# A two-layer encoder trunk on one core: where the modulation sums, the head's small rows and the last expert unit's combine are done

## The chip, the cores and the metric

The kernel runs on 1 core of one Trainium2 chip. The metric is the device time of one execution in microseconds (us), as the median of several runs. Engines are called as in the profile: PE (TensorE), DVE (VectorE), ACT (ScalarE), POOL (GpSimd), SP (SyncE, which here only issues DMAs); PEld is PE's weight load.

## What is computed

A sequence of 512 tokens with 1024 channels goes through two layers. Each layer has a mixer (layer 0: multi-scale pooling beside banded chunk attention; layer 1: a Mamba-2 state-space mixer with 8 groups) and a mixture of 32 experts, of which each token takes two. Every sub-layer is modulated by six rows of 1024 numbers, `mod`, which depend on one conditioning vector `c`. The reference, cut to what matters here:

```python
c_act = jax.nn.silu(c)                                   # (1, 1024)
for layer in range(2):
    mod = c_act @ ada_w[layer] + ada_b[layer]            # 1024 x 6144 weights
    shift1, scale1, gate1, shift2, scale2, gate2 = split(mod, 6)
    h = rmsnorm(x, norm1_w[layer]) * (1 + scale1) + shift1
    if layer == 0:
        u, q, k, v = split(h @ mix_w_in)
        mix = concat([pool_mixer(u), chunk_attention(q, k, v, rel_bias)]) @ mix_w_out
    else:
        mix = mamba2_mixer(h, ssm_w_in, conv_w, conv_b, dt_bias, A_log, D_skip, norm_w, w_out)
    x = x + gate1 * mix
    h2 = rmsnorm(x, norm2_w[layer]) * (1 + scale2) + shift2
    g = top-1 of softmax(h2 @ w_group + b_group)         # 4 groups of 8 experts
    w = top-2 of softmax of the logits inside group g    # two experts a token
    x = x + gate2 * sum_e w_e * (silu(h2 @ w1_e) * (h2 @ w3_e)) @ w2_e
return rmsnorm(x, final_norm_w)
```

## The kernel before

**The stages in order.** Head (x is loaded and normalized, the shift and scale of layer 0 are summed, the V columns of attention are formed); even mixer (scores, softmax, pooling, beside the Q, K and U columns, one 128-column strip at a time); output product and router; experts of layer 0 in 17 units; combine of layer 0, in which the last expert results are added to x, x is normalized and transposed into `sh_hi`, `sh_lo`, the input of layer 1; the SSM, 8 groups `g0` to `g7`, each of which forms the columns b, c, x, z of its group (PSUM tiles `pdb`, `pdc`, `pdx`, `pdz`), convolves them on DVE (`cvx`), and runs the scan (`pst`, `pyd`, `pyo`; `ms` are the decay masks); output product and router; experts of layer 1; combine and final norm.

**Modulation sums.** `ada(layer, part, eng)` (L164) forms 2048 numbers of `mod`: for each of 8 blocks `k` of 128 rows, a 1 MB tile `ada` of weights is loaded by SP into a ring of 5 buffers (tag w8), DVE multiplies it by column `k` of silu(c), `ccol`, and adds it to the running sum (L189), in place; then four matmuls with a stationary of ones (L198, PSUM tile `pada`) add over the 128 partitions, each into 32 partitions of one bank. It is a generator: each `yield` lets the caller put the next round where it wants. Five parts are formed so: (0,1), (0,2), (1,0) in the even mixer (table FILL says how many rounds go behind each piece of work) and (1,1), (1,2) in the SSM (list `fill`). The part (0,0) is formed in the head in two halves of 512 numbers twice (`ada_sums(b)`, L564), and the first four channels' blocks of h need half 0, the other four half 1 (`modulate(b)`).

**Head.** V products go in pairs of k: `wsplit` makes a high part of the weight on ACT and a low part on the engine of table LO ("v": POOL). `late_loads()` (L271) has SP load a zero row and three vectors of 32 numbers, each spread over 128 partitions: `dcol` (from ssm_D, with a stride of two elements, two DMAs), `dtb`, `arow`. Behind them in SP's queue stands `wq`, the first strip of Q columns, whose buffer is that of the V weights `vr4`.

**Experts and combine.** A unit u is 128 slots of one or two experts: PE forms `ph` and `pyy`, DVE scales the result into `y`, which SP stores to DRAM rows `yd`. The units of LAST and the overflow unit are not stored: their results are split in a high and a low half (`yh`, `yl`) and added to x by one-hot matmuls (`products`, L1073, operand `yot` or `yo`, PSUM tile `pyc`) and DVE adds (`padd`, L1086). The operand of unit 13 takes part in step u = 15 of the loop, those of 14 and 15 in `combine`. The stored results come back as 8 indirect DMAs of POOL that add into x (`ygather`, L1174, issued in unit GAT = 15). `combine` then follows an order written out by hand (STEPS; x0: add tile 0, h0: next step of its normalization, w1: split a weight). In layer 0 the call `ahead()` (L1433) ahead of it has SP load `wdt`, the 32 dt columns of the SSM weight, split on ACT and DVE into `whl`.

Of the kernel before, what the change touches and what calls it, by code (L numbers as in the profile page):

```python
# [20 lines left out]
P = 128  # L21
T = 512
# [14 lines left out]
GAT = 15  # L37
# [16 lines left out]
HOLD = 7  # L54
PINS = 3
# [7 lines left out]
LO = {"v": "G", "e": "VVG", "m": "V", "o": "GVV", "s": "VV"}  # L63
# [4 lines left out]
STEPS = "x0 h0 x1 h1 h0 x2 h2 h0 h1 x3 h2 h3 h3 h0 h1 h2 h1 w1 h3 w2 h3 h2"  # L68
# [7 lines left out]
def trunk_kernel(ctx, tc, x, c, ada_w, ada_b, norm1_w, norm2_w, mix_w_in, pool_w, pool_scale,  # L76
# [86 lines left out]

    def ada(layer, part, eng, first=None):  # L164
# [19 lines left out]
        load(1)  # L184
        for k in range(KD):
# [8 lines left out]
        for _ in range(SLACK):  # L194
            yield
        p = ps(name=f"pada{layer}{part}")
        for q in range(4):
            PE.matmul(p[32 * q:32 * q + 32, :], ones[:, 0:32], ws[KD - 1][:, q * 512:(q + 1) * 512], start=True,  # L198
                      stop=True, skip_group_check=True)
# [71 lines left out]
    def late_loads():  # L271
        SP.dma_start(yd[len(MAIN) * P:, :], zrow)
        for q in range(2):
# [216 lines left out]
    def even_mixer(layer):  # L490
        with ExitStack() as es:
# [15 lines left out]
            def ada_loads(b):  # L507
                SP.dma_start(adb[0:64:32, b * 512:(b + 1) * 512], dap(ada_b, b * 512, [[D, 2], [1, 512]]))
                for k in range(0, KD, 2):
# [3 lines left out]
                    aw[b, k], aw[b, k + 1] = (t[:, d].rearrange("p q n -> p (q n)") for d in range(2))  # L513
# [27 lines left out]
            def modulate(b):  # L541
# [12 lines left out]
            def v_products(b):  # L554
                for kk in (4 * b, 4 * b + 2):
# [8 lines left out]
            def ada_sums(b):  # L564
                V.tensor_scalar(aw[b, 0], aw[b, 0], ccol[:, 0:1], None, op0=ALU.mult)
                for k in range(1, KD):
                    V.scalar_tensor_tensor(aw[b, k], aw[b, k], ccol[:, k:k + 1], aw[b, k - 1], op0=ALU.mult,
                                           op1=ALU.add)
                p = ps(name=f"pada00{b}")
                for q in range(2):  # L570
                    PE.matmul(p[32 * q:32 * q + 32, :], ones[:, 0:32], aw[b, KD - 1][:, q * 512:(q + 1) * 512],
                              start=True, stop=True, skip_group_check=True)
                m = adb[0:64, b * 512:(b + 1) * 512]
                V.tensor_add(m, p[0:64], m)
                p = ps((P, 4, 64), name=f"pm00{b}")
                for q in range(4):
                    PE.transpose(p[:, q, :], m[:, q * P:(q + 1) * P], ident[0:64, 0:64])
                ks = slice(4 * b, 4 * b + 4)
                V.scalar_tensor_tensor(ab[:, 0, 0, ks], p[:, :, 32], 1.0, n1w[0][:, ks], op0=ALU.add, op1=ALU.mult)
                V.tensor_copy(ab[:, 0, 1, ks], p[:, :, 0])  # L580
# [3 lines left out]
            late_loads()  # L584
# [5 lines left out]
            v_products(1)  # L590
# [117 lines left out]
            adas = [ada(0, 1, V), ada(0, 2, V), ada(1, 0, V)]  # L708
# [81 lines left out]
    class Moe:  # L790
# [282 lines left out]
        def products(self, i, parts):  # L1073

            ps2 = [ps(name=f"pyc{self.layer}{i}{hf}") for hf in range(2)]
            for hf, p in enumerate(ps2):
                for n, part in enumerate(parts):
                    for q in range(2):
                        PE.matmul(p, part[2][:, i * P:(i + 1) * P], part[hf][:, q * 512:(q + 1) * 512],  # L1079
                                  start=n + q == 0, stop=n == len(parts) - 1 and q == 1)  # L1080
            return ps2
# [6 lines left out]
        def run(self, before_end=None):  # L1088
# [30 lines left out]
            def results(u, between=None):  # L1119
# [3 lines left out]
                             self.parts_y[max(u - NPAIR + 2, 0)] if last(u) else None)  # L1123

            ts = {}
            for u in range(NPAIR + 1):
# [20 lines left out]
                if 1 < u < NPAIR and last(u - 2):  # L1147
                    for i in range(NT):
                        self.padd(i, self.products(i, self.parts_y[:1]))
# [8 lines left out]
                if u == GAT:  # L1158
                    self.ygather()
                    for n in range(2):  # L1160
                        t = we([P, 2, 2 * T], F32R, f"yl{n}_{layer}")
                        o = we([P, 2, 2 * T], F32R, f"yo_{layer}")[:, 0, 0:T] if n else ot[:, T:2 * T]
                        self.parts_y.append((t[:, 0], t[:, 1], o))
                if u == 1:
# [256 lines left out]
    def odd_mixer(layer, prev):  # L1421
        with ExitStack() as es:
# [10 lines left out]
            def ahead():  # L1433
                dense.first = prev.gathers[HOLD]
                dense.load(2)
                w = prev.y_tile("wdt")
                wdt.append(w[:, 0:256].rearrange("p (k c) -> p k c", k=KD))
                SP.dma_start(wdt[0], w_in[:, 6144:6176].rearrange("(k p) c -> p k c", p=P))
                wdt.append(ws4(F32R, "whl")[:, 0:512].rearrange("p (k c) -> p k c", k=KD))
# [365 lines left out]
```

## Time and profile before

| | us |
|---|---|
| median of 3 runs | 1119.99 |
| lowest and highest run | 1119.96, 1123.87 |
| the profiled execution's own time | 1120.03 |
| its span in the trace | 1118.3 |
| PE busy in the span | 973.2 |
| DVE busy in the span | 800.3 |

The profiled execution's time is 1.7 us more than its span and 0.04 us from the median. Over the span PE is busy 87%, DVE 72%, ACT 35%, POOL 27%; the mean granted clock of TensorE is 0.932 of full speed, that is, it is at 1.2 GHz instead of 2.4 GHz in part of the span.

### The profile page before, as it was taken

What the parts mean: (1) busy time and instruction counts of PE and PEld (TensorE: products, weight loads), DVE (VectorE), ACT (ScalarE), POOL (GpSimd) and SP (SyncE); (2) the same over time, 40 slices, a digit from 0 to 9 for tenths busy, and PEclk for the clock granted to TensorE, in tenths of its full rate; (3) what the DMA queues carried; (4) which work ended last, traced back from release to release, by engine and by line L of the source; (5) the groups of instructions that cost most, each with busy time, mean ns of one, the idle gap of its engine ahead of it and who ended that gap; (6) DMA issues with size and microseconds to landing.
All of it is one profiled execution on the core that took longest, in us unless ns stands there. A gap on an engine that the chain in (4) does not pass through costs nothing. (4 is left out here: it accounts for less than half of the span.)

```text
span 1118.3 us, 15578 instructions
## 1 busy us (share of the span) xinstructions
PE 973.2 (87%) x5474; PEld 729.5 (65%) x5474; DVE 800.3 (72%) x1650; ACT 388.9 (35%) x753; POOL 300.2 (27%) x329
## 2 busy tenths in 40 slices
PE   4588788699699996898999899899989999799994
PEld 3466466388556654776786777777766878556653
DVE  6717986654565874789997989887797555564976
ACT  3135332425123232433444333443433325222332
POOL 4413100204231122411513416244142004231124
PEclk9789888799799998899999999999999999799997
DMA  9476876598699979536473465554334945699987
GB/s 332 139 265 168 286 282 252 215 364 330 209 364 414 411 229 255 210 107 198 143 264 88 135 194 159 190 158 113 126 109 152 333 154 209 204 390 415 412 278 185
DMA packets 140200, 263.88 MB, mean 236 GB/s; under 512 B 19917, under 2 KB 82337, under 8 KB 134994
## 3 DMA queue, kind: packets, MB, share of 16 engines
q1 hardware_dynamic: 129122, 235.40, 60.1%
q0 software_dynamic: 8928, 20.97, 7.2%
q10 hardware_dynamic: 2064, 6.42, 1.4%
q8 instruction: 47, 0.77, 0.3%
q14 instruction: 39, 0.32, 0.1%
HBM read 254.19 MB, written 20.11 MB: 245 GB/s over the span
## 5 line engine op out<-in xcount | busy, mean ns | idle before, releaser
L1036 PE MATMUL ph<-w,xT 128*64 128x256 f32 (+1 forms) x1152 | 132.1, 374 | 0.9 <-DVE xT L1020 0.7
L1036 PEld LDWEIGHTS ph<-w,xT 128*64 128x64 f32 x1152 | 86.8, 139 | 51.8 <-issue 10.9
L189 DVE SCALAR_TENSOR_TENSOR ada<-ada,ccol,ada 128x2048 f32<-128x2048 f32 x35 | 87.1, 2489 | 0.2
L1003 POOL DMA_INDIRECT xg<-xnd,toks x32 | 32.3, 1008 | 149.8 <-PE pxt L1015 122.6
L1057 PE MATMUL pyy<-w,hidT 128*64 128x512 f32 x272 | 65.9, 605 | 4.2 <-ACT hidT L1049 4.2
L1038 ACT ACTIVATE th<-ph 128x128 f32<-128x128 f32 x34 | 9.4, 278 | 160.8 <-PE pht L1047 137.1
L1022 ACT ACTIVATE xT<-pxt,mc 128x128 f32<-128x128 f32 x136 | 51.3, 458 | 17.9 <-PE pxt L1015 10.9
L1062 DVE SCALAR_TENSOR_TENSOR y<-pyy,wsl,gate 128x512 f32<-128x512 f32 x68 | 48.1, 744 | 6.1 <-DMA yd<-y 4.5
L1015 PE MATMUL pxt<-ident,xg 128*128 128x128 f32 x272 | 37.9, 284 | 15.5 <-DVEq L1383 7.9
L1086 DVE TENSOR_TENSOR x<-x,pyc 128x512 f32<-128x512 f32 x64 | 40.4, 682 | 14.1 <-PE pyc L1079 8.0
L1039 DVE SCALAR_TENSOR_TENSOR th<-th,ph 128x128 f32<-128x128 f32 x34 | 9.8, 287 | 55.7 <-ACT th L1038 55.7
L1020 DVE TENSOR_SCALAR xT<-pxt,mc 128x128 f32<-128x128 f32 x136 | 46.6, 405 | 1.4 <-PE pxt L1015 1.4
L1581 DVE TENSOR_SCALAR ms<-lb,acs 128x128 f32<-128x128 f32 x128 | 41.0, 359 | 5.9 <-DMA lb<-acd 3.6
L1015 PEld LDWEIGHTS pxt<-ident,xg 128*128 128x128 f32 x272 | 34.5, 194 | 16.2 <-issue 15.6
L1548 DVE SCALAR_TENSOR_TENSOR cvx<-pdx,cw,cvx 128x511 f32<-128x511 f32 (+2 forms) x48 | 35.4, 738 | 6.7 <-ACT cvx L1545 6.6
L1178 POOL DMA_INDIRECT x<-yd,row x16 | 25.1, 1571 | 50.0 <-DMA xgfw<-in_final_norm_w_dram 22.3
L1584 POOL TENSOR_TENSOR ms<-ms,cbm 128x512 f32<-128x512 f32 x16 | 32.0, 2001 | 17.8 <-ACT ms L1583 16.0
L1057 PEld LDWEIGHTS pyy<-w,hidT 128*64 128x64 f32 x272 | 16.5, 136 | 28.1 <-issue 19.4
L1079 PE MATMUL pyc<-yh,yot 128*128 128x512 f32 x128 | 33.7, 398 | 1.0 <-DVE yot L1070 1.0
L469 DVE TENSOR_TENSOR sor<-sor,gate 128x1024 f32<-128x1024 f32 x16 | 20.4, 1276 | 18.0 <-DMA sor<-in_ssm_w_out_dram 17.9
L661 ACT ACTIVATE scs<-scs,mx 128x512 f32<-128x512 f32 (+3 forms) x32 | 17.7, 555 | 36.2 <-DVE mx L660 32.8
L1079 PEld LDWEIGHTS pyc<-yh,yot 128*128 128x128 f32 x128 | 23.4, 188 | 9.6 <-issue 1.9
(1074 smaller groups left out, 2778.4 us busy)
## 6 DMA issues: line engine op xcount, KB each, us to landing
w<-in_moe_w_dram SPq DMA_DIRECT2D x192, 512.0 KB
ada<-in_ada_w_dram SPq DMA_DIRECT2D x40, 1024.0 KB
yd<-y SPq DMA_DIRECT2D x22, 512.0 KB
ada<-in_ada_w_dram SPq DMA_DIRECT2D x16, 512.0 KB
wx<-in_ssm_w_in_dram SPq DMA_DIRECT2D x16, 512.0 KB
wz<-in_ssm_w_in_dram SPq DMA_DIRECT2D x16, 512.0 KB
lb<-acd SPq DMA_DIRECT2D x32, 256.0 KB
sor<-in_ssm_w_out_dram SPq DMA_DIRECT2D x16, 512.0 KB
```

The lines of the kernel that those rows point to most:

```text
L189: a = eng.scalar_tensor_tensor(ws[k], ws[k], ccol[:, k:k + 1], ws[k - 1], op0=ALU.mult, op1=ALU.add)
L1003: d = GP.indirect_dma_start(out=xg, out_offset=None, in_=xnd[:, :], in_offset=bass.IndirectOffsetOnAxis(ap=idx, axis=0), bounds_check=T - ...
L1015: PE.transpose(p[:, q, :], xv[:, 4 * hf + q, :], ident)
L1020: V.tensor_scalar(xT[:, k, :], p[:, q, :], a, b, op0=ALU.mult, op1=ALU.add)
L1022: S.activation(xT[:, k, :], p[:, q, :], AF.Identity, bias=b, scale=a)
L1036: PE.matmul(ph[64 * j:64 * j + 64, n:n + h, :], xT[:, k, 64 * j:64 * j + 64], w13[n][:, :, k, :], start=k == 0, stop=k == KD - 1, skip_gro ...
L1057: PE.matmul(py[64 * j:64 * j + 64], hT[:, 64 * j:64 * j + 64], w2[:, s], start=True, stop=True, skip_group_check=True)
L1062: V.scalar_tensor_tensor(y[:, s], py, self.wsl[:, slot:slot + 1], self.gate2[:, s], op0=ALU.mult, op1=ALU.mult)
L1079: PE.matmul(p, part[2][:, i * P:(i + 1) * P], part[hf][:, q * 512:(q + 1) * 512], start=n + q == 0, stop=n == len(parts) - 1 and q == 1)
L1086: V.tensor_add(xst["x"][i][:, s], xst["x"][i][:, s], p)
L1548: V.scalar_tensor_tensor(a[:, sh:], p[:, :T - sh], cw[:, tap, ch:ch + 1], a[:, sh:], op0=ALU.mult, op1=ALU.add)
L1581: V.tensor_scalar(ms[:, h, :], lb[:, h, :], acs[:, cq, 4 * g + h:4 * g + h + 1], 0.0, op0=ALU.subtract, op1=ALU.min)
```

## The change

All modulation sums go to PE. A round k is four matmuls whose stationary is column k of `ccol`, broadcast to 32 columns, and whose moving operand is the loaded tile; they accumulate in the same PSUM bank from round 0 to round 7. DVE has no round any more. In the head the halves accumulate the same way, with the two k of a pair in different partitions, so one add more is needed behind the transposes. The vectors `dcol`, `dtb`, `arow` are loaded as three rows of [1, 32] into `hrow`, spread by one matmul with ones and copied by DVE (`head_rows`). The low parts of the V weights and all `hlo` go to DVE. The operand of unit 13 moves from step u = 15 to the final products, which become 64 matmuls in place of 48, and begin with three of the four operands for tiles 0 and 1; the gathers are issued in unit 14; in layer 0 `wdt` is loaded in unit 10 and split on ACT and POOL as a step `w0` of the combine.

```diff
-GAT = 15
+GAT = 14
+EARLY = 10
-LO = {"v": "G", "e": "VVG", "m": "V", "o": "GVV", "s": "VV"}
+LO = {"v": "V", "e": "VVG", "m": "V", "o": "GVV", "s": "VV"}
-STEPS = "... h3 h0 h1 h2 h1 w1 h3 w2 h3 h2"
+STEPS = "... h3 h0 h1 h2 h1 w0 w1 h3 w2 h3 h2"
+    def ada_mm(p, k, w, first, last):
+        for q in range(4):
+            PE.matmul(p[32 * q:32 * q + 32, :], ccol[:, k:k + 1].to_broadcast([P, 32]), w[:, q * 512:(q + 1) * 512],
+                      start=first, stop=last, skip_group_check=True)
...
+            if not eng:
+                if not k:
+                    p = ps(name=f"pada{layer}{part}")
+                ada_mm(p, k, ws.pop(k), k == 0, k == KD - 1)
+                continue
...
     def late_loads():
         SP.dma_start(yd[len(MAIN) * P:, :], zrow)
-        for q in range(2):
-            SP.dma_start(dcol[64 * q:64 * q + 64, :], dap(ssm_D, q, [[0, 64], [2, 16]]))
-        SP.dma_start(dtb, dap(ssm_dt_bias, 0, [[0, P], [1, 32]]))
-        SP.dma_start(arow, dap(ssm_A_log, 0, [[0, P], [1, 32]]))
+        hrow = st_.tile([1, 3, 32], F32, name="hrow")
+        for n, src in enumerate((ssm_D, ssm_dt_bias, ssm_A_log)):
+            SP.dma_start(hrow[:, n, :], dap(src, 0, [[0, 1], [1, 32]]))
...
-                    (V if g % 2 else GP).tensor_sub(parts[1][g], xa[g], parts[0][g].bitcast(F32))
+                    V.tensor_sub(parts[1][g], xa[g], parts[0][g].bitcast(F32))
...
             def ada_sums(b):
-                V.tensor_scalar(aw[b, 0], aw[b, 0], ccol[:, 0:1], None, op0=ALU.mult)
-                for k in range(1, KD):
-                    V.scalar_tensor_tensor(aw[b, k], aw[b, k], ccol[:, k:k + 1], aw[b, k - 1], op0=ALU.mult,
-                                           op1=ALU.add)
                 p = ps(name=f"pada00{b}")
-                for q in range(2):
-                    PE.matmul(p[32 * q:32 * q + 32, :], ones[:, 0:32], aw[b, KD - 1][:, q * 512:(q + 1) * 512],
-                              start=True, stop=True, skip_group_check=True)
+                for k in range(0, KD, 2):
+                    for d in range(2):
+                        for q in range(2):
+                            o = 64 * d + 32 * q
+                            PE.matmul(p[o:o + 32, :], ccol[:, k + d:k + d + 1].to_broadcast([P, 32]), aw[b, k][:, d, q],
+                                      start=k == 0, stop=k == KD - 2, skip_group_check=True)
...
-            adas = [ada(0, 1, V), ada(0, 2, V), ada(1, 0, V)]
+            adas = [ada(0, 1, None), ada(0, 2, None), ada(1, 0, None)]
...
-                             self.parts_y[max(u - NPAIR + 2, 0)] if last(u) else None)
+                             self.parts_y[max(u - NPAIR + 3, 0)] if last(u) else None)
...
-                if 1 < u < NPAIR and last(u - 2):
+                if 1 < u < NPAIR - 1 and last(u - 2):
...
-                p = [self.products(i, self.parts_y) for i in range(NT)]
+                p = self.products((0, 1), self.parts_y[:-1], False)
+                p = self.products((0, 1), self.parts_y[-1:], True, p)
+                p += self.products((2, 3), self.parts_y, True)
...
-                split(wdt[1][:, :, 0:32], wdt[1][:, :, 32:64], wdt[0], V)
+                split(wdt[1][:, :, 0:32], wdt[1][:, :, 32:64], wdt[0], GP)
...
-                a11, a12 = ada(1, 1, V, prev.gathers[HOLD]), ada(1, 2, V, prev.gathers[HOLD])
+                a11, a12 = ada(1, 1, None, prev.gathers[HOLD]), ada(1, 2, None, prev.gathers[HOLD])
```

What SP has in its queue in the head, behind the last V weights, before:

```order
L272 DMA yd<-zrow 1x1024
L274 DMA dcol<-in_ssm_D_dram 64x16x1 x2
L275 DMA dtb<-in_ssm_dt_bias_dram 128x32
L276 DMA arow<-in_ssm_A_log_dram 128x32
L402 DMA wq_498<-in_mix_w_in_dram 128x8x128
```

and now:

```order
L286 DMA yd<-zrow 1x1024
L289 DMA hrow<-in_ssm_D_dram 1x32
L289 DMA hrow<-in_ssm_dt_bias_dram 1x32
L289 DMA hrow<-in_ssm_A_log_dram 1x32
L425 DMA wq_522<-in_mix_w_in_dram 128x8x128
```

The four DMAs that write 128 partitions have become three that write one; `wq` stands behind them as before.

On PE, in the even mixer before the second U strip (`pdu` are the U columns): before, no sum stands here, and the first of the three parts has one row, behind the scores `sc` of a later strip:

```order
L655 MATMUL sc_965<-kT_891,qT_836 128x128
L655 MATMUL sc_974<-kT_891,qT_836 128x128
L198 MATMUL pada_983<-ada_732,ones 32x512 x4
L637 MATMUL py_1010<-pl_772,pw 128x512
L426 MATMUL pdq_1022<-hhi_176,q2h 128x512
```

Now five rounds of that part stand between the two U strips (the other three follow one at a time):

```order
L452 MATMUL pdu_709<-hhi_179,u0l 128x512
L168 MATMUL pada_743<-ada_697,ccol 32x512 x4
L168 MATMUL pada_743<-ada_699,ccol 32x512 x4
L168 MATMUL pada_743<-ada_701,ccol 32x512 x4
L168 MATMUL pada_743<-ada_748,ccol 32x512 x4
L168 MATMUL pada_743<-ada_754,ccol 32x512 x4
L449 MATMUL pdu_780<-hhi_176,u1h 128x512
```

On PE at the end of SSM group g0, where group g1's b columns (`pdb`) follow, before:

```order
L1612 MATMUL pst_4974<-xw_4912,btk_4900 128x256
L1612 MATMUL pst_4977<-xw_4912,btk_4900 128x256
L1612 MATMUL pst_4981<-xw_4912,btk_4900 128x256
L426 MATMUL pdb_5022<-sh_hi,b1h 128x512
L428 MATMUL pdb_5022<-sh_lo,b1h 128x512
```

and now, with three rounds of part (1,1) in between:

```order
L1651 MATMUL pst_5046<-xw_4981,btk_4969 128x256
L1651 MATMUL pst_5050<-xw_4981,btk_4969 128x256
L168 MATMUL pada_5072<-ada_5066,ccol 32x512 x4
L168 MATMUL pada_5072<-ada_5068,ccol 32x512 x4
L168 MATMUL pada_5072<-ada_5070,ccol 32x512 x4
L449 MATMUL pdb_5101<-sh_hi,b1h 128x512
```

Each row with x4 is one round. Further groups of rounds stand at the ends of g2 (5), g3 (2), g4 (4) and g6 (2).

## Rows read from the trace of the kernel before

**Rows 1.** Busy time by stage: the stretch, its length, then busy us (instructions) of PE, PEld, DVE, ACT and POOL, the granted TensorE clock, the busy share of the DMA engines and GB/s. The stretches are: head (second part), even mixer, experts of layer 0, its combine, the SSM, the combine of layer 1.

```profile
20.40:85.70 65.30, 42.83 (x160) 31.26 (x160) 29.27 (x30) 17.91 (x23) 20.27 (x8) 0.79 0.66 227
85.70:221.20 135.50, 108.37 (x500) 76.38 (x500) 108.72 (x223) 52.53 (x128) 23.44 (x20) 0.86 0.69 241
...
295.80:422.80 127.00, 124.75 (x928) 77.56 (x928) 85.07 (x230) 37.86 (x108) 31.56 (x28) 1.00 0.93 340
422.80:465.10 42.30, 29.35 (x147) 25.15 (x146) 26.14 (x57) 17.02 (x35) 17.00 (x19) 0.80 0.89 277
...
505.70:838.20 332.50, 306.30 (x1570) 244.14 (x1568) 293.60 (x452) 129.09 (x187) 116.63 (x80) 0.96 0.51 157
...
1080.00:1118.30 38.30, 22.41 (x116) 13.71 (x114) 26.19 (x57) 12.73 (x32) 18.94 (x17) 0.85 0.73 167
```

**Rows 2.** What PE waited for in the even mixer (85.7 to 221.2 us): the waiting row's tile and line, what released it, us in total, times, longest.

```profile
PE pada L198 <- DVE ada L189: 9.1, 1, 9.1
PE sc L655 <- DVE c L111: 6.7, 1, 6.7
PE pdu L426 <- DVE mx L658: 3.9, 2, 2.0
PE pdq L426 <- DVE mx L658: 3.4, 1, 3.4
```

**Rows 3.** The same for the SSM (505.7 to 838.2 us).

```profile
PE pxd L1598 <- DVE cvx L1552: 17.9, 7, 4.1
PE pyd L1631 <- DVE ms L1584: 8.3, 4, 3.7
```

**Rows 4.** The rounds of the sums on DVE, from the page's costliest groups: how many, busy us, mean ns of one, idle time ahead of them.

```profile
L189 DVE SCALAR_TENSOR_TENSOR ada<-ada,ccol,ada 128x2048 f32<-128x2048 f32 x35 | 87.1, 2489 | 0.2
```

**Rows 5.** The four matmuls of one part on PE (tile pada alone), in two stretches: columns PE, PEld and DVE busy (instructions), granted clock of the stretch, DMA share, GB/s. The four appear as eight instructions.

```profile
120.00:140.00 20.00, 1.93 (x8) 0.20 (x8) 0.69 (x1) 0.74 0.75 270
...
780.00:800.00 20.00, 1.07 (x8) 0.16 (x8) 0.68 (x1) 1.00 0.35 115
```

**Rows 6.** The same four in PE's timeline, with the next strip behind them: start, us, engine, line, operation, tiles, shapes.

```profile
647.48 1.07 PE L198 MATMUL pada<-ada,ones 128*32 128x512 f32 x8
648.48 0.50 PE L426 MATMUL pdb<-sh_hi,b4h 128*128 128x512 f32 x1
```

**Rows 7.** DVE's rounds by SSM group: the stretch, its length, busy us of line 189 alone (instructions), clock, DMA share, GB/s; groups g0, g2 and g3.

```profile
505.70:555.40 49.70, 10.46 (x4) 0.93 0.59 180
...
601.40:648.50 47.10, 0.00 (x0) 0.96 0.36 101
648.50:692.30 43.80, 10.80 (x5) 1.00 0.68 206
```

**Rows 8.** What PE waited for in the second part of the head (20.4 to 85.7 us).

```profile
PE pdq L426 <- ACT q0h L110: 7.4, 1, 7.4
PE accv L434 <- ACT hhi L549: 5.6, 1, 5.6
PE pada L571 <- DVE ada L567: 4.9, 1, 4.9
```

**Rows 9.** SP's queue in the head, and ACT's first split of a Q strip (start, us, in brackets the idle time ahead and its releaser).

```profile
30.99 3.52 SPq L274 DMA_DIRECT2D dcol<-in_ssm_D_dram  x2
34.56 3.66 SPq L275 DMA_DIRECT2D dtb<-in_ssm_dt_bias_dram  x1
...
41.09 4.32 SPq L402 DMA_DIRECT2D wq<-in_mix_w_in_dram  x1
...
58.99 1.06 ACT L110 ACTIVATE q0h<-wq 128x1024 fp32r<-128x1024 f32 x1 [13.02 <-DMA wq<-in_mix_w_in_dram]
```

**Rows 10.** DMA in the head: the stretch, its length, PE, PEld, DVE, ACT, POOL, clock, DMA share, GB/s.

```profile
24.00:36.00 12.00, 3.80 (x10) 1.22 (x10) 9.87 (x11) 4.65 (x6) 7.47 (x3) 0.54 1.05 386
38.00:46.00 8.00, 8.00 (x27) 6.41 (x28) 7.86 (x5) 1.06 (x1) 3.06 (x1) 0.75 0.05 0
...
56.00:60.00 4.00, 0.00 (x0) 0.00 (x0) 0.00 (x0) 1.01 (x2) 0.00 (x0) 0.50 0.87 237
```

**Rows 11.** The combine of layer 0 in the timelines of SP, ACT, DVE, PE and POOL.

```profile
417.17 0.38 SPq L1438 DMA_DIRECT2D wdt<-in_ssm_w_in_dram  x1
...
435.05 0.42 ACT L110 ACTIVATE whl<-wdt 128x256 fp32r<-128x256 f32 x1 [10.75 <-DMA wdt<-in_ssm_w_in_dram]
...
435.50 0.43 DVE L111 TENSOR_TENSOR whl<-wdt,whl 128x256 fp32r<-128x256 f32 x1 [9.45 <-ACT whl L110]
435.84 2.47 DVE L1086 TENSOR_TENSOR x<-x,pyc 128x512 f32<-128x512 f32 x4
...
440.78 3.78 PE L350 MATMUL pt<-xh,x 128*128 128x128 f32 x16 [6.25 <-DVE xh L347]
...
409.34 1.60 POOL L1178 DMA_INDIRECT x<-yd,row  x1 [19.25 <-DVE x L1086]
```

**Rows 12.** The matmuls pyc alone: unit 13's, and the final ones of layer 0 (columns as in group 5).

```profile
406.00:412.00 6.00, 3.94 (x16) 2.92 (x16) 4.05 (x7) 1.00 0.12 12
422.70:434.60 11.90, 11.67 (x48) 8.85 (x48) 0.00 (x0) 1.00 1.00 191
```

**Rows 13.** The first gather of layer 1 on POOL, and the first and last add behind a gather on DVE.

```profile
1081.47 1.60 POOL L1178 DMA_INDIRECT x<-yd,row  x1 [22.31 <-DMA xgfw<-in_final_norm_w_dram]
...
1098.70 1.28 DVE L1086 TENSOR_TENSOR x<-x,pyc 128x512 f32<-128x512 f32 x2 [4.06 <-DMA x<-yd,row]
```

More of the change, by code (lines that the diff above doesn't have):

```diff
@@ L193, in ada @@
                 tc.keep_in_program_order(a)
-        for _ in range(SLACK):
+        for _ in range(SLACK if eng else 0):
             yield
[L196 to L199, printed above, removed]
+        if eng:
+            p = ps(name=f"pada{layer}{part}")
+            for q in range(4):
+                PE.matmul(p[32 * q:32 * q + 32, :], ones[:, 0:32], ws[KD - 1][:, q * 512:(q + 1) * 512], start=True,
+                          stop=True, skip_group_check=True)
         m = b
@@ L1071, in results, with products @@
                                     op0=ALU.add, op1=ALU.is_equal)
[L1073 to L1077, printed above, removed]
-                    for q in range(2):
-                        PE.matmul(p, part[2][:, i * P:(i + 1) * P], part[hf][:, q * 512:(q + 1) * 512],
-                                  start=n + q == 0, stop=n == len(parts) - 1 and q == 1)
-            return ps2
+        def products(self, tiles, parts, stop=True, sums=None):
+            out = sums or [[ps(name=f"pyc{self.layer}{i}{hf}") for hf in range(2)] for i in tiles]
+            for i, ps2 in zip(tiles, out):
+                for hf, p in enumerate(ps2):
+                    for n, part in enumerate(parts):
+                        for q in range(2):
+                            PE.matmul(p, part[2][:, i * P:(i + 1) * P], part[hf][:, q * 512:(q + 1) * 512],
+                                      start=not sums and n + q == 0, stop=stop and n == len(parts) - 1 and q == 1,
+                                      skip_group_check=True)
+            return out
         def padd(self, i, ps2):
@@ L1159, in run @@
                     self.ygather()
[L1160 to L1162 removed]
+                    wide = [wp.tile([P, 2048], F32R, tag="w8", name=f"y{n}_{layer}", bufs=W8) for n in ("l0", "oh")]
+                    y = [wide[0].rearrange("p (h n) -> p h n", h=2)]
+                    y += [we([P, 2, 2 * T], F32R, f"yl{n}_{layer}") for n in (1, 2)]
+                    for t, o in zip(y, (ot[:, T:2 * T], wide[1][:, 0:T], wide[1][:, T:2 * T])):
                         self.parts_y.append((t[:, 0], t[:, 1], o))
+                if u == EARLY and early:
+                    early()
                 if u == 1:
@@ L1435, in ahead, with early, splits @@
                 dense.load(2)
-                w = prev.y_tile("wdt")
-                wdt.append(w[:, 0:256].rearrange("p (k c) -> p k c", k=KD))
+            def early():
+                wdt.append(small.tile([P, KD, NLOG], F32, tag="wr", name="wdt", bufs=1)[:, :, 0:32])
                 SP.dma_start(wdt[0], w_in[:, 6144:6176].rearrange("(k p) c -> p k c", p=P))
+            def splits(n):
+                if n:
+                    return dense.split(n, GP)
                 wdt.append(ws4(F32R, "whl")[:, 0:512].rearrange("p (k c) -> p k c", k=KD))
-                split(wdt[1][:, :, 0:32], wdt[1][:, :, 32:64], wdt[0], V)
-            prev.run(ahead)
+                split(wdt[1][:, :, 0:32], wdt[1][:, :, 32:64], wdt[0], GP)
+            prev.run(ahead, early)
             with ExitStack() as es2:
@@ L1451, in after @@
                     yield from hT_tile(layer, i, h_hi, h_lo)
-                prev.combine([after(i) for i in range(NT)], STEPS, lambda n: dense.split(n, GP))
+                prev.combine([after(i) for i in range(NT)], STEPS, splits)
                 prev.close()
```

41 lines of the change are left out of this document (27 added, 14 removed).

## The prediction

> **What bounds the kernel now.** I read the stages first, then what PE waited for in each, then the timelines around the waits. In the table by stage [rows 1] PE is busy 98% of the experts of layer 0 (124.75 of 127.00 us) and 92% of the SSM (306.30 of 332.50), but 80% of the even mixer (108.37 of 135.50), 66% of the head's second part (42.83 of 65.30) and 69% of the combine of layer 0 (29.35 of 42.30). So PE is the bound, more or less everywhere: work put on PE costs its own time where PE is full, and is free only where it fills a wait. The clock column says what waiting costs beside: at 0.86 in the even mixer TensorE runs at 1.2 GHz for (1-0.86) x 2 x 135.5 = 38 us, in the head's second part for 27 us, in the combine for 17 us, and in the SSM, at 0.96, for 27 of 332.5 us. The waits of the even mixer come to 27.1 us, of which 9.1 are for DVE's last modulation round, 6.7 for a DVE split (tile `c`) and 7.3 for the softmax maximum `mx` [rows 2]. The SSM's come to 26.2: 17.9 for the x convolution, once in each of seven groups, and 8.3 for the masks `ms` [rows 3]. DVE is busy 88% of the SSM and 80% of the even mixer, but it is PE's idle time that a relief of DVE can give back, not DVE's.
>
> **What a round costs.** On DVE 35 of the 40 rounds took 87.1 us, 2.49 us each, with 0.2 us of idle time ahead of them in all [rows 4]: they never waited for a load. On PE the trace has no round, but it has four matmuls of the same shape, 32 columns by 512, which end each part: 1.07 us at full clock, 1.93 at half clock [rows 5]. In place, the next strip begins 1.00 us behind their start [rows 6]. A round is taken as 1.0 us at full clock; the operands are float32 as before, and only the stationary is another. The Trainium skill, "TensorEngine Tiling (Array Packing)", section "Key Properties", says that a change of tiling mode drains TensorE while tiles of one mode are independent. By that rule the edges of the 1.07 us would be paid once for a group of rounds, not once for each, and a round inside a group would be nearer to 0.9; the forty would cost some 4 us less, an estimate. No row here shows two rounds in a row, so the sum keeps 1.0.
>
> **Even mixer.** Removed: 24 rounds of DVE (21 at 2.49 us, and the first of each part, which only multiplies: 52 us at least of its 108.72), and the three closing quadruples on PE; added: 24 rounds on PE, so +21 us at full clock. Removed with it: the wait of 9.1 us for the last sum and, since DVE then is half empty, the 6.7 us for `c` [rows 2]. The half clock also mattered: of 38 us at 1.2 GHz PE was busy between 11 (all idle time inside) and 30 (idle spread evenly), and half of that is lost, 5 to 15 us; I take 12, because the waits are what precede the low stretches. With most waits gone I leave 4. Work at full clock 108.4 - 12 = 96, plus 21, plus 4 of clock, plus what is left of the waits: 27.1 - 9.1 - 6.7 = 11.3, less half of the 7.3 for `mx`, since that is one DVE queue with fewer rounds ahead, 8. That makes 129 to 130 against 135.5: **-6**. Bounds: all of `mx` gone and the clock full throughout, with rounds at 0.85, gives -15; both other waits merely replaced, and the clock as before, gives +6.
>
> **SSM.** The rounds of DVE stand in g0, g1, g3, g4 [rows 7]. If they were on the path, groups with them would be longer. They aren't: g3 with 10.80 us of rounds is 43.8 us long, g2 with none 47.1. So their removal gives little by itself, and 16 rounds on PE less two quadruples cost +14. What they can give back are the waits for `ms` that come just behind DVE's rounds, two of the four, about 7 of 8.3 us [rows 3], and the low clock that follows such gaps, of which I take 4 (27 us at half clock, half of it lost at most, 13). The 17.9 for `pxd` I leave: they stand in every group, with rounds or without. **+3**; bounds -5 (a third of the `pxd` waits goes too) and +12 (nothing of the waits is recovered).
>
> **Head.** PE waits 7.4 us for the first Q split, 5.6 for `hhi`, 4.9 for the sum of DVE [rows 8]. The split waits for `wq`, issued at 41.09, which lands only by 58.99 [rows 9]. It isn't bandwidth: the DMA engines carry 386 GB/s at 24 to 36 us, then are busy 0.05 at 38 to 46 while `wq` has been issued, and carry 237 GB/s at 56 to 60 [rows 10]. Ahead of `wq` in the queue stand `dcol` (2048 pieces of one number) and `dtb`, with 3.5 us each for their issue alone [rows 9]. I read this as a few rings working through small pieces, with `wq` behind them. The Trainium skill, "DMA: Bandwidth & Descriptors", says in its section on descriptors that one descriptor moves one contiguous run of the last dimension; `dcol` is the case with a run of one element, and the trace agrees with it in that 8 us pass at 0.05. With three rows of 32 numbers instead, `wq` lands some 5 us behind its issue, at about 46, before PE is done with the V products, and the 7.4 are gone. The 4.9 are gone too: the first four rounds run as the tiles land. Against that, the second half's four rounds in place of one row, 3 to 6 us (taken 4.5), and 5.5 us less of half clock cost, being 27 us at half clock whose share under work, 0.66, is halved: 9 lost now, 3.5 left. With DVE's rounds out of its queue the chain to `hhi` gets shorter; I count 1 for it. Sum -7.4 - 4.9 + 4.5 - 5.5 - 1 = -14; because `wq`'s buffer now comes free behind a DVE step that stands behind the second half's sum, I take **-12**. Bounds -18 (the 5.6 go as well) and -3 (`wq`'s buffer comes free 9 us later).
>
> **Combine of layer 0.** SP issues `wdt` at 417.17 and it lands with 435.05, behind the gathers; ACT and DVE split it, and only behind that split, at 435.84, DVE's in-order queue gets to the adds of tile 0; PE waits 6.25 us for it, until 440.78 [rows 11]. With `wdt` there since unit 10 the adds of tile 0 can run as soon as its products and its gathers are there. Unit 13's 16 matmuls cost 3.94 us in step 15 and cost the same behind the loop, 16 x 11.67 / 48 = 3.9 [rows 12]: the last product ends at 434.6 as before, and the gathers, whose first waited at 409.34 for DVE's adds of unit 13 [rows 11], come somewhat earlier, since those adds are gone from there. So the transposes can start at 434.6 in place of 440.78, -6, and the stage's 17 us at half clock shrink, -2: **-8**. Bounds -12 and -3 (a late gather takes the place of `wdt`).
>
> **End.** The gathers of layer 1 start at 1081.47 and DVE's first add follows at 1098.70, with PE long done [rows 13]. They can't start before the last stored rows are in DRAM, so an earlier issue gives **-0.5** (0 to -2). The expert units stay as they are.
>
> **Sum.** -12 - 6 + 3 - 8 - 0.5 = -23.5. The profiled execution took 1120.03 us, as good as the median of 1119.99, so 1096.5; I say **1097**.
>
> **The rivals.** (1) Waits aren't recovered: both mixers at their upper bounds, +6 and +12, the rest as above: 1120 - 12 + 18 - 8 - 0.5 = 1117.5. For it: the `mx` and `pxd` waits are chains of several engines [rows 2, 3]; against: 9.1 us wait for the very rounds removed. (2) The head gives only 3: 1106. For it: the buffer of `wq`; against: DVE has the head's 16 rounds less ahead of that step. (3) DVE's relief is worth more: mixers at -15 and -5: 1080. For it: DVE at 80 and 88% [rows 1]; against: g2, with no rounds, is no shorter [rows 7]. (4) Slower: PE's queue is in order and now holds the rounds, so a weight tile that lands late stops everything behind it. DVE's 0.2 us of idle time [rows 4] says that tiles came in time for DVE's slower pace, but the buffers are freed by PE's order now, in bursts of up to five rounds from a ring of five. It decides from a mean wait of (23.5 + 5.6) / 40 = 0.7 us a round; at 1.0 us it gives 1136.
>
> **How the numbers follow.** Forecast 0.54, (1) 0.16, (2) 0.11, (3) 0.13, (4) 0.06. The range takes in (2) and most of (1) and (3): 1082 to 1117. A measurement of this kernel can tell some 0.5%, 5.6 us, from no change: faster is below 1114.4. Half of (1), and a little of the others, fall between 1114.4 and 1125.6. Faster 0.85, same 0.09, slower 0.06.
>
> **What would show it.** Right: no wait of PE for `ada` from DVE; `pada` rows of about 1.0 us in groups; `q0h` on ACT before 52; no `whl` on DVE, and `pt` directly behind `pyc`; PE busier and the clock above 0.93. Wrong: a wait of `pada` for DMA; a new wait for `mx`, `ms` or `cvx` as long as the old; the SSM longer than 336 us with its waits unchanged; `wq` issued after 50.

## The result, and the profile after

| | before | changed |
|---|---|---|
| median, us | 1120.91 | 1093.91 |
| ratio, 95% interval | | 0.9748 (0.972 to 0.9777) |
| span of the profiled execution, us | 1118.3 | 1092.1 |
| PE busy, DVE busy, us | 973.2, 800.3 | 991.4, 680.5 |
| mean granted clock | 0.932 | 0.965 |

The changed kernel is 27 us faster; 1097 had been said. The medians are over four executions each and the ratio over the fast ones: one of the changed kernel took 2525 us, and one of the kernel with both combine parts undone, below, 1277. A second measurement of the changed kernel, beside the experiments, gave 0.9763 (0.9727 to 0.9799), 1094.06 us. PE has 18 us more of work and DVE 120 us less.

The same table by stage as [rows 1], in the changed kernel (stretch, its length, busy us of PE, PEld, DVE, ACT, POOL, clock, DMA share, GB/s): head, even mixer, experts of layer 0, its combine, the SSM, experts of layer 1, the combine of layer 1.

```profile
20.70:75.10 54.40, 45.09 (x219) 31.13 (x219) 18.79 (x34) 19.88 (x24) 3.12 (x3) 0.94 0.77 264
75.10:201.76 126.66, 119.67 (x669) 74.75 (x669) 53.59 (x199) 50.87 (x125) 21.62 (x20) 0.99 0.75 264
...
273.30:400.50 127.20, 123.48 (x923) 77.48 (x925) 84.22 (x247) 38.58 (x110) 29.45 (x27) 0.98 0.92 342
400.50:440.10 39.60, 33.63 (x183) 29.05 (x180) 26.62 (x53) 16.46 (x35) 20.62 (x22) 0.87 1.03 308
...
478.80:812.40 333.60, 313.95 (x1681) 243.90 (x1679) 256.04 (x436) 130.13 (x188) 108.98 (x80) 0.98 0.51 156
...
931.60:1050.00 118.40, 116.14 (x873) 73.49 (x872) 75.42 (x223) 34.55 (x101) 21.57 (x21) 0.98 0.98 379
1050.00:1092.10 42.10, 25.14 (x129) 16.45 (x127) 24.92 (x54) 12.56 (x32) 19.44 (x17) 0.86 0.72 172
```

The head's second part is 54.4 us long where it had 65.3, the even mixer 126.7 where it had 135.5, the SSM 333.6 against 332.5. PE's busy time rose in both mixers by much less than the rounds' work (11.3 us in the even mixer, 7.7 in the SSM), because the clock rose with it, from 0.86 to 0.99 and from 0.96 to 0.98. The experts of layer 1 and their combine must be taken together: 160.5 us, against 121.4 and 38.3 (159.7) before.

What PE waited for in the changed kernel: in the head, in the even mixer, and in the SSM (as in [rows 2, 3, 8]):

```profile
PE accv L457 <- ACT hhi L572: 4.9, 2, 4.4
PE pm L599 <- DVE adab L596: 1.0, 1, 1.0
PE accv L459 <- DVE hlo L573: 0.7, 1, 0.7
...
PE pm L306 <- DVE adab L215: 3.1, 1, 3.1
PE sc L682 <- ACT kT L723: 2.7, 1, 2.7
PE py L664 <- DVE pl L659: 1.7, 1, 1.7
PE po L711 <- ACT ptT L702: 1.0, 1, 1.0
PE pada L168 <- DMA ada<-in_ada_w_dram: 1.0, 1, 1.0
...
PE pxd L1637 <- DVE cvx L1591: 17.7, 7, 4.2
PE pyd L1670 <- DVE ms L1623: 1.9, 2, 1.1
```

In the even mixer the waits for `ada`, `c` and `mx` are all gone; 9.5 us of others are left of 27.1. In the SSM the 8.3 for `ms` shrank to 1.9 and the 17.9 for the x convolution stayed. A round waited for a late weight tile once, 1.0 us.

What rounds cost on PE, in its timeline (start, us): five in a row, and a single one, each with the strip behind it.

```profile
83.16 4.50 PE L168 MATMUL pada<-ada,ccol 128*32 128x512 f32 x40
87.59 0.50 PE L449 MATMUL pdu<-hhi,u1h 128*128 128x512 f32 x1
...
95.21 1.06 PE L168 MATMUL pada<-ada,ccol 128*32 128x512 f32 x8
96.20 0.50 PE L449 MATMUL pdq<-hhi,q1h 128*128 128x512 f32 x1
```

Five take 4.50 us, 0.90 each; a single one 1.06.

### The profile page after: what moved, and what is told of

Its sections match the earlier page's. It is cut to its first block, busy times and chain, and to the rows that moved or that the text cites. A ratio compares the mean times of both kernels' runs of the same rounds, so it can differ in the third digit from the quotient of the medians.

```text
span 1092.1 us, 16191 instructions
## 1 busy us (share of the span) xinstructions
PE 991.4 (91%) x5812; PEld 725.9 (66%) x5812; DVE 680.5 (62%) x1591; ACT 389.5 (36%) x753; POOL 275.2 (25%) x324
## 5 line engine op out<-in xcount | busy, mean ns | idle before, releaser
L1620 DVE TENSOR_SCALAR ms<-lb,acs 128x128 f32<-128x128 f32 x128 | 35.9, 330 | 18.9 <-PE pyd L1670 14.5
L1115 DVE TENSOR_TENSOR x<-x,pyc 128x512 f32<-128x512 f32 x48 | 30.4, 682 | 20.8 <-DMA x<-yd,row 15.8
L168 PE MATMUL pada<-ada,ccol 128*32 128x512 f32 x320 | 39.7, 598 | 1.0 <-DMA ada<-in_ada_w_dram 1.0
L1622 ACT ACTIVATE ms<-ms 128x512 f32<-128x512 f32 x32 | 19.9, 626 | 30.5 <-DVE ms L1620 30.2
L1623 POOL TENSOR_TENSOR ms<-ms,cbm 128x512 f32<-128x512 f32 x16 | 25.5, 1599 | 15.6 <-ACT ms L1622 8.3
L1107 PE MATMUL pyc<-yh,yot 128*128 128x512 f32 x96 | 25.8, 397 | 1.8 <-DVE yot L1097 1.8
L1681 DVE SCALAR_TENSOR_TENSOR zt<-zt,pdz 128x512 f32<-128x512 f32 x16 | 10.9, 683 | 25.9 <-ACT zt L1680 25.9
```

What stands on the lines that cost most here:

```text
L168: PE.matmul(p[32 * q:32 * q + 32, :], ccol[:, k:k + 1].to_broadcast([P, 32]), w[:, q * 512:(q + 1) * 512], start=first, stop=last, skip_gr ...
L1115: V.tensor_add(xst["x"][i][:, s], xst["x"][i][:, s], p)
L1620: V.tensor_scalar(ms[:, h, :], lb[:, h, :], acs[:, cq, 4 * g + h:4 * g + h + 1], 0.0, op0=ALU.subtract, op1=ALU.min)
```

## The experiments

All kernels but one start from the changed kernel and undo one part. Ratios are to the kernel before, run beside them; the changed kernel is at 0.975 to 0.976 on this scale. The ratios' intervals are 0.3 to 0.7% to either side. The spans are those of the profiled executions (changed: 1092.1 and, a second time, 1093.7), and single executions scatter: nine of the changed kernel span 1089.5 to 1097.5 us. So a trace tells where time lies, but a difference of a few us between two spans is not the size of an effect; the medians and ratios are held against it.

**The head's small loads as before.**

```diff
-        hrow = st_.tile([1, 3, 32], F32, name="hrow")
-        for n, src in enumerate((ssm_D, ssm_dt_bias, ssm_A_log)): ...
+        for q in range(2):
+            SP.dma_start(dcol[64 * q:64 * q + 64, :], dap(ssm_D, q, [[0, 64], [2, 16]]))
+        SP.dma_start(dtb, ...)
+        SP.dma_start(arow, ...)
```

> The changed kernel with the head's three vectors loaded as before (two DMAs of single numbers for dcol, then dtb and arow, each to 128 partitions), everything else as changed. The prediction's reading, that wq's 7.4 us wait was the small pieces ahead of it in the queue, taken alone: q0h on ACT at 57 to 60 again, and 5 to 8 us slower than the changed kernel, 1099 to 1102. The rival, from the changed kernel's trace: the V products now all stand ahead of the Q strip and end at 61.5, while q0h is there at 49.2, so 10 us of lateness would be hidden: within 2 us of the changed kernel's 1094, with q0h late all the same.

Measured: 1104.61 us, ratio 0.987 (0.9843 to 0.9897), span 1099.7. SP's queue, and ACT, in this kernel:

```profile
31.19 4.69 SPq L288 DMA_DIRECT2D dcol<-in_ssm_D_dram  x2
35.93 3.23 SPq L289 DMA_DIRECT2D dtb<-in_ssm_dt_bias_dram  x1
...
44.47 0.38 SPq L416 DMA_DIRECT2D wq<-in_mix_w_in_dram  x1
45.89 8.07 SPq L416 DMA_DIRECT2D wk<-in_mix_w_in_dram  x1
...
59.13 1.06 ACT L111 ACTIVATE q0h<-wq 128x1024 fp32r<-128x1024 f32 x1 [9.66 <-DMA wq<-in_mix_w_in_dram]
...
74.92 1.06 ACT L111 ACTIVATE u1h<-wu 128x1024 fp32r<-128x1024 f32 x1 [6.15 <-DMA wu<-in_mix_w_in_dram]
79.27 1.06 ACT L111 ACTIVATE q1h<-wq 128x1024 fp32r<-128x1024 f32 x1 [3.29 <-DMA wq<-in_mix_w_in_dram]
80.23 0.58 ACT L713 ACTIVATE kT<-pdk 128x512 f32<-128x512 f32 x1
```

and the first scores on PE, here and then in the changed kernel:

```profile
80.86 1.22 PE L672 MATMUL sc<-kT,qT 64*128 64x512 f32 x2 [8.64 <-ACT kT L713]
```

```profile
75.10 1.13 PE L682 MATMUL sc<-kT,qT 64*128 64x512 f32 x4 [2.68 <-ACT kT L723]
```

The loads alone account for 5.8 us at the first scores and 7.6 at the end of these two executions, and for 10.7 in the medians. `wq` is issued at the same time in both (44.47 and 44.32), and what the DMA engines do behind that is different (stretch, its length, busy us of PE, PEld, DVE, ACT and POOL, clock, DMA share, GB/s; here, then in the changed kernel):

```profile
46.00:54.00 8.00, 7.17 (x32) 5.56 (x30) 3.40 (x6) 3.42 (x4) 0.00 (x0) 1.00 0.14 26
54.00:60.00 6.00, 6.00 (x28) 4.99 (x27) 0.00 (x0) 0.87 (x1) 0.00 (x0) 1.00 0.79 203
```

```profile
44.30:49.20 4.90, 4.62 (x21) 3.45 (x19) 2.76 (x9) 3.30 (x4) 0.26 (x1) 1.00 0.62 177
```

In the changed kernel `wq` is issued and split at these times:

```profile
44.32 0.39 SPq L425 DMA_DIRECT2D wq<-in_mix_w_in_dram  x1
...
49.22 1.04 ACT L111 ACTIVATE q0h<-wq 128x1024 fp32r<-128x1024 f32 x1
```

Neither theory had the way: `wq` is 10 us late again and, as the rival says, the V products cover that (PE's wait ahead of `pdq` is 0.3 us). But everything behind `wq` in the queue is late too: `wk` takes 8.07 us to issue, `wu` and the next `wq` come later, ACT waits for them in its order, and `kT`, whose product was done long before, stands behind those splits. PE pays at the scores, 8.64 us in place of 2.68.

**The three rows alone, in the kernel before.** The same edit the other way round, in the kernel before.

> The kernel before with the three rows alone: hrow, one matmul and DVE's copies in place of dcol, dtb, arow. The prediction's reading of the head, that the 7.4 us wait for q0h is wq behind the small pieces: wq lands by 48, q0h before 50, and 5 to 8 us faster than before, 1112 to 1115. The rival, that DVE's sums, which end with half 1 at 51 to 53, hold the Q strip anyway: q0h early but 0 to 2 us faster.

Measured: 1115.66 us, ratio 0.9946 (0.9915 to 0.9976), span 1114.2, 4.1 us under before. ACT's split there:

```profile
52.27 1.06 ACT L110 ACTIVATE q0h<-wq 128x1024 fp32r<-128x1024 f32 x1 [4.38 <-PE accv L444]
```

It waits no longer for a DMA but for PE to free its place; `wq` is in time. The 7.4 us wait is gone, but part of it comes back: PE waits 6.9 us for DVE's sum where it waited 4.9, and 2.1 ahead of `pdq` for a step of DVE (`pu`). Of the 7.4 us some 4 to 5 are won: 4.0 at the first scores (81.7 against 85.7), 4.7 in the medians (the kernel before had 1120.37 beside it).

**The head's own sums on DVE.** `ada_sums` as before, all else as changed.

> The changed kernel with the head's own two half sums on DVE as before; rows, V splits and all other parts as changed. The head was 10.6 us shorter in the trace, and the run with the old small loads gave back 7 of them (5.8 at the first scores). What is left for the sums is 3 to 5 us: 3 to 5 us slower than the changed kernel, with PE waiting for the first half's sum again. The rival, that the V products' cover hides it: 0 to 1 us.

Measured: 1090.7 us, ratio 0.9749 (0.9696 to 0.9802), span 1087.2: not slower, contrary to the expectation. PE's waits at the head:

```profile
PE pada L594 <- DVE ada L590: 4.9, 1, 4.9
PE accv L457 <- ACT hhi L572: 4.3, 2, 3.8
```

The 4.9 us wait for DVE's sum is back, yet the V products end at the same time (61.5 in both timelines): PE is spared the work of the rounds. The first scores stand 1.3 us earlier (73.8 against 75.1), hardly outside the 74.3 to 76.7 of the eight traces whose head is the changed kernel's. On PE or on DVE, the head's sums come out about even; the medians differ by 3.2 us, the ratios' intervals overlap, and the span's 4.9 us are within the scatter of single executions.

**Low parts on POOL.** Table LO ("v") and every second `hlo` as before.

> The changed kernel with the low parts of the V weights and every second hlo back on POOL. The prediction counted about 1 us for it in the head: 1 to 3 us slower, with PE waiting for hlo of POOL again. The rival: POOL is free and DVE has no rounds to be slowed, so no difference.

Measured: 1097.22 us, ratio 0.9792 (0.9754 to 0.983), against 0.9763 of the changed kernel beside it; span 1095.0. PE waits for POOL again:

```profile
PE accv L459 <- POOL hlo L573: 2.9, 2, 1.6
```

The first scores stand at 78.3, behind all of those eight traces and 3.2 us behind the changed kernel's. The medians differ by 3.2 us as well; the ratios' intervals overlap.

**The even mixer's sums on DVE.**

```diff
-            adas = [ada(0, 1, None), ada(0, 2, None), ada(1, 0, None)]
+            adas = [ada(0, 1, V), ada(0, 2, V), ada(1, 0, V)]
```

> The changed kernel with the three parts of the even mixer summed on DVE as before. The forecast's term says 6 us slower than changed (1100); the stage of the changed kernel, 126.7 us in place of 135.5, says 9 (1103). The rival, that the stage is shorter because it begins earlier with its loads further ahead, and not for the sums: 0 to 2 us.

Measured: 1100.71 us, ratio 0.9827 (0.9798 to 0.9857), span 1098.7, 6.6 us over the changed kernel's. The even mixer and PE's longest waits in it:

```profile
76.70:207.60 130.90, 105.51 (x501) 74.52 (x501) 107.02 (x222) 51.07 (x126) 23.25 (x19) 0.88 0.72 252
...
PE pada L212 <- DVE ada L202: 7.7, 1, 7.7
PE sc L682 <- DVE c L112: 6.5, 1, 6.5
PE pdq L449 <- DVE mx L685: 5.8, 1, 5.8
...
PE pdu L449 <- DVE mx L685: 1.9, 1, 1.9
```

All three waits are back at the old size, those for `mx` too, and the clock is at 0.88. So these waits, and with them the low clock, were DVE's rounds, and the 24 rounds on PE cost less than they give.

But the stage is not back at its old length. From the first scores to the first output product (`mo`) it takes 130.9 us here, 126.7 in the changed kernel (124.0 to 128.0 in the eleven traces that have its sums on PE), 135.5 in the kernel before, and 132.5 (81.7 to 214.2) in the kernel before with the three rows alone. So some 4 of the stage's 8.8 us are the sums'. Another 3 come with the head's three rows, which touch nothing in this stage: the rival, that the stage gains from what stands ahead of it, holds for about half, though how it does isn't shown.

**The SSM's sums on DVE.**

```diff
-                a11, a12 = ada(1, 1, None, ...), ada(1, 2, None, ...)
+                a11, a12 = ada(1, 1, V, ...), ada(1, 2, V, ...)
```

> The changed kernel with the two parts of the state-space layer summed on DVE as before. The forecast's term (+3 for PE's rounds) says 3 us faster than the changed kernel, 1091. The stage's length, 333.6 us in place of 332.5 in the two traces with a gain of 4 us in g1 and losses in g3, g5 and g7, says no difference within 1.5 us. The rival, that relief of DVE is worth more than the rounds cost PE: slower by 3 or more, and waits for ms back at 8 us.

Measured: 1093.66 us, ratio 0.9769 (0.9744 to 0.9795), span 1091.3: no difference. From the first `pdb` to the last `pyo` the layer takes 381.1 us, against 382.8 in the changed kernel and 383.1 before. The waits for `ms` are back, those for the convolution as ever:

```profile
PE pxd L1637 <- DVE cvx L1591: 18.5, 7, 4.1
PE pyd L1670 <- DVE ms L1623: 8.8, 5, 3.7
```

**Each round of the SSM twice.** The sums of parts (1,1) and (1,2) come out doubled; what follows behind the SSM computes with other numbers and is not read.

```diff
+                for r in range(1 + (layer == 1 and part > 0)):
+                    ada_mm(p, k, t, k + r == 0, k == KD - 1 and r == (layer == 1 and part > 0))
```

> The changed kernel with each of the 16 rounds of the state-space layer done twice (the sums of parts (1,1) and (1,2) come out doubled), to measure what a round costs in its place. If a round costs its 0.9 to 1.0 us on PE: the layer 15 to 16 us longer. If rounds partly fill PE's waits there, as it seems from the layer being only 1.1 us longer than before with 14 us more of work: 8 us or less.

Measured: 1108.21 us, ratio 0.9876 (0.9837 to 0.9916), span 1107.9. The tile `pada` alone in the SSM, with 16 rounds (changed) and with 32 (here):

```profile
478.80:812.40 333.60, 14.77 (x128) 3.65 (x128) 1.38 (x2) 0.98 0.51 156
```

```profile
478.30:827.60 349.30, 28.50 (x256) 7.80 (x256) 1.37 (x2) 0.98 0.49 151
```

Sixteen rounds more are 13.7 us more of PE, 0.86 each, and the SSM ends 13.5 us later in the two timelines (last `pyo` at 827.6 against 814.1; the second stretch above ends with it, the first 1.7 us ahead of it). So a round costs its full time, here too; that the first sixteen cost nothing on balance means that they won as much elsewhere.

**Both parts of the combine undone, and each alone.** For `wdt`: loaded by `ahead()` into a result tile of the expert stage, split on ACT and DVE, no step w0. For unit 13: GAT 15, its product in step 15.

> The changed kernel with both parts of the combine undone: wdt loaded behind the loop and split on ACT and DVE, and unit 13's product in step 15, the gathers in unit 15. In the run that undid wdt alone SP issued wdt at 388.4, ahead of the gathers, because the result buffers came free earlier without unit 13's product, and PE's 6.25 us wait did not return. If that is so, either part is enough to remove the wait, and only with both undone does it return: pt 6 us behind the last pyc, wdt landing behind the gathers, and 6 to 9 us slower than the changed kernel. The rival, that the wait of before came from elsewhere: within 2 us of the changed kernel.

> The changed kernel with wdt loaded behind the gathers and split on ACT and DVE ahead of the combine, as before. The forecast's term: 6 to 8 us slower than the changed kernel, 1100 to 1102, with DVE's first add of tile 0 behind whl again. The rival, that the gathers bind the combine anyway: 0 to 2 us.

> The changed kernel with unit 13's product in step 15 and the gathers in unit 15 as before; wdt stays early. The forecast's terms (PE's work only moves, the end gives 0.5): within 1.5 us of the changed kernel, pt directly behind pyc. The rival, that the gathers are late without it and bind the combine: 3 us or more slower, with DVE's first add waiting for a gather.

| undone | us | ratio | span |
|---|---|---|---|
| wdt alone | 1097.64 | 0.9801 (0.977 to 0.9832) | 1096.2 |
| unit 13 alone | 1098.38 | 0.9811 (0.9759 to 0.9863) | 1092.4 |
| both | 1103.8 | 0.9852 (0.9783 to 0.992) | 1101.1 |

With both undone the wait of before is there again, ACT waiting for `wdt` and PE for the transposes' operand:

```profile
417.03 0.42 ACT L111 ACTIVATE whl<-wdt 128x256 fp32r<-128x256 f32 x1 [11.65 <-DMA wdt<-in_ssm_w_in_dram]
...
422.74 1.65 PE L373 MATMUL pt<-xh,x 128*128 128x128 f32 x6 [7.73 <-DVE xh L370]
```

With `wdt` alone undone `pt` follows `pyc` at once. The difference is in SP's queue:

```profile
388.37 0.38 SPq L1472 DMA_DIRECT2D wdt<-in_ssm_w_in_dram  x1
```

```profile
SPq L1472 <- DMA yd<-y: 9.2, 1, 9.2
```

```profile
398.25 0.38 SPq L1471 DMA_DIRECT2D wdt<-in_ssm_w_in_dram  x1
```

```profile
SPq L1471 <- DVE yh L112: 18.6, 1, 18.6
```

The first two are the kernel with `wdt` alone undone (SP's timeline, and what SP waited for ahead of that load), the others that with both. The load's place is a result tile, and whether it comes free with a store or with a later split, 10 us on, decides whether `wdt` goes ahead of the eight gathers or behind the first five. So either part of the change removes the wait of PE ahead of `pt`. It does not follow that the second adds nothing to the first: in the medians each part undone costs some 4 us (3.7 for `wdt`, 4.5 for unit 13) and both 9 to 10, as if each gave a share of its own. The span of 1092.4 for unit 13 is the shortest of four, the others being 1096.4 to 1097.6, so its trace has nothing of that loss in it, and between the expectation and its rival the run doesn't decide. The 4.1 of the span for `wdt` don't lie in the combine, where its transposes begin 1.9 us earlier than in the changed kernel, but behind it, in the SSM and the second experts. What makes either loss is open.

**Rounds on PE in the even mixer alone.** As undoing the sums of the head and of the SSM cost nothing, both are on DVE again here, the rest as changed.

> The changed kernel with the sums of the head and of the state-space layer on DVE again, and those of the even mixer on PE. The two undone parts alone came out at 0.9749 and 0.9769 of before, with spans of 1087.2 and 1091.3 where the changed kernel had 1092.1. If PE's rounds pay only in the even mixer: 1 to 6 us faster than the changed kernel run beside it. The rival, that these are differences of the clock's phase and no more: the same within 2 us.

> The changed kernel again, so that the kernels beside it can be held against it on the same chip: 0.972 to 0.978 of before, span 1090 to 1093.

Measured side by side: 1092.74 us, ratio 0.9746 (0.9717 to 0.9775), span 1086.9, against 1094.06 us, 0.9763 (0.9727 to 0.9799), span 1093.7. The medians are 1.3 us apart, which lies in the expected range and in the rival's, and the intervals overlap, so this isn't shown to be better; it does as well as the changed kernel with 24 of the mixers' 40 rounds on PE and none of the head's.

## Why the prediction was right

The sum was -23.5; in spans it came to -26.2, in the medians to -27.0. The waits that it named are gone, and most of them for the reason that it gave. That the sum came so near is in part luck: terms were missed to both sides, and where an experiment takes a term alone its size is not always what the stage gained. Point by point, by the two timelines:

**Head, -12 said, -10.6 at the first scores.** The cause named was right: with the three rows `q0h` runs at 49.22 in place of 58.99, and undoing them costs 5.8 us at the first scores. The way was only half right. The 0.05 at 38 to 46 us [rows 10], taken as a sign of small pieces, doesn't tell by itself, since the changed kernel shows 0.05 there too, with `wq` not yet issued; the run with the old loads does, 0.14 where the changed kernel has 0.62. In the new order `q0h` is not what PE would wait for; the lateness goes down the queue to the strips behind, and through ACT's order to `kT`. The wait of 4.9 for the sum is gone, and set off by the rounds of the second half, as said: undone, they change the head by 1.3 us. The clock's term held: 0.94 in place of 0.79 is (1-0.94) x 2 x 54.4 = 6.5 us at 1.2 GHz, from 27, and with PE busy 0.83 of the stretch 2.7 us lost, where 3.5 were left. The 1 counted for `hhi` came as 0.7 (5.6 to 4.9). For the low parts that left POOL the sum has no term at all; undone, they cost 3.2 at the first scores. Rival (2), the buffer of `wq`, came only in small: issued at 44.32, in place of 41.09, 3.2 us later and not 9. Rows, POOL and sums, 5.8 + 3.2 - 1.3, are 7.7 of the 10.6 us; the rest isn't taken apart. One edit in it is told neither in the section on the change nor in the sum: in the kernel before, the V products went ahead of the second half's sum for four of the eight k, now for two (`v_products(0)`, then `v_products(2)` and `v_products(4, 6)` behind it). No run undoes that alone.

**Even mixer, -6 said, -8.8 measured, some 4 of them by the sums.** The price of the rounds was right, and the waits nearly. The rounds' work: 24 on PE, 24.94 us of `pada` less three old quadruples, as said 21. The waits for `ada` and `c` went as said; those for `mx`, of which I left half, went wholly, and the run with DVE's rounds brought them back, 7.7 us. The low clock shrank to (1-0.99) x 2 x 126.66 = 2.5 us at 1.2 GHz, at most 1.3 lost, where 4 were left. What the sum did not have is that the stage gains from the head: with the same waits back it is still 4.6 us shorter than before, 3.0 of them with the head's three rows alone. So -6 is between what the sums gave the stage, -4, and what the stage gained; the near figure is not a confirmation of the term's size.

**SSM, +3 said, about 0 measured.** Its stretch is 1.1 us longer; against the groups' own marks, from the first `pdb` to the last `pyo`, it is 0.4 shorter. The terms hold one by one: the rounds cost 14.77 us, 0.86 to 0.92 each and not 1.0; `ms` gave back 6.4 of the 7 said; `pxd` nothing; the clock 0.96 to 0.98 gives at most half of 13 us, 6.5, where 4 were said. The argument from g2 and g3, that groups with rounds on DVE are no longer than one without, did not show that these rounds were free: put back, they bring 6.9 us of waits for `ms` with them. What the run that put them back shows is that their cost there is about that of the rounds on PE, 1.7 us less by the marks from `pdb` to `pyo`, so the sign of +3 may well be right for this term alone.

**Price of a round.** On the row of a single quadruple, 1.07, I took 1.0. By the Trainium skill, "TensorEngine Tiling (Array Packing)", "Key Properties", the drain is paid for a change of mode, and the traces agree: five rounds in a row take 4.50 us, a single one 1.06, that is about 0.2 for the edges and 0.86 a round; that the 0.2 is a drain isn't shown. Of the 4 us by which that rule would have lowered the sum, 1.6 fall to the SSM, where 14.77 for sixteen rounds in five groups is 1.2 under the price taken; in the even mixer, where half of the 24 rounds stand singly, 24.94 is not under it.

**Combine, -8 said, about -7 measured.** The wait of 6.25 is gone: `pt` stood 6.25 us behind the last `pyc`, and now follows it at once; from the experts' first product to the first `pdb` it is 157.8 us, from 164.7:

```profile
415.44 1.08 PE L1107 MATMUL pyc<-yl,yoh 128*128 128x512 f32 x4
416.35 1.95 PE L373 MATMUL pt<-xh,x 128*128 128x128 f32 x16
```

The wrong step is the attribution. I gave the gain to `wdt` and nothing to unit 13; either of them removes the wait, through SP's queue, and in the medians each undone costs about as much as the other.

**End, -0.5 said, about +1 measured.** Layer 1's last sixteen products went from step 15 to the end, and the experts' last `pyy` ends 30.3 us earlier than before, where their first product was 27.3 earlier; but the end comes only 26.2 earlier. What binds it, as said, are the gathers behind the last store (1043.80, before 1070.17); the first gather starts 10.9 us behind the store's issue, before 11.3, though the profile doesn't name the store as its releaser:

```profile
1043.80 0.33 SPq L1094 DMA_DIRECT2D yd<-y  x1
...
1054.72 1.60 POOL L1210 DMA_INDIRECT x<-yd,row  x1 [22.19 <-issue]
...
1072.84 1.28 DVE L1115 TENSOR_TENSOR x<-x,pyc 128x512 f32<-128x512 f32 x2 [9.13 <-DMA x<-yd,row]
```

DVE's first add now waits 9.13 us for a gather, where it waited 4.06 [rows 13]: the 3 us gained by PE are given back there, and one more.

**Rivals.** Rival (4) had the right place: one round did wait for a tile, 1.0 us in all, far from the 0.7 a round from which it decides. Rival (1) is excluded by the waits, rival (3) was half so: the even mixer gave more, the SSM not.

What stays open: in spans the single undos add up to 7.6 + 2.9 + 6.6 + 9.0 (rows, POOL, even mixer, combine) = 26.1 less 0.8 and 4.9 for what costs (SSM, head's sums), 20.4; in medians to 10.7 + 3.2 + 6.8 + 9.1 = 29.8 less 0.3 and 3.2, 26.3; the change measured 26.2 and 27.0. Whether the parts add up or share some us the experiments don't tell, since each is known to some 3 us at best.

## What to carry to other kernels

Work moved onto the bounding engine can pay where that engine idles at low clock waiting for the helper: read the gain from the waits that name the helper, add the clock that they cost, and subtract the full price of the work, since the experiment with doubled rounds shows no discount. A helper that is 88% busy is not by that a limit: in the SSM its extra work cost about what the same work costs on PE, and moving it gave nothing on balance. A load that is late in an in-order queue may show its price at an operand three places further on, and two edits may each remove the same wait, so undo them alone and together before naming the one that did it, and hold the trace of each against its other executions: a wait that is gone is not yet the time.

## What the runs showed of the hardware

Four small DMAs that spread three vectors of 32 numbers over 128 partitions held up the 512 KB load behind them by some 10 us (issued at 44.47 and used at 59.13, against 44.32 and 49.22), with the DMA engines little busy (0.14 at 46 to 54 us in the run with the old loads); as three rows of one partition they don't. Which of the four does it, the strided `dcol` or the broadcasts, no run tells. Four 32-column matmuls of 512 float32 columns cost 0.86 us together inside a group, and a group costs about 0.2 us more where it stands between full-width ones, an estimate from the rows of 4.50 and 1.06 us that fits the sixteen rounds of the SSM (16 x 0.86 + 5 x 0.2 = 14.8, measured 14.77).
